# The four z projections of a hybrid block, moved ahead of v heads 1 to 4

## Chip, cores and metric

One Trainium2 chip, one of its cores. The metric is the device time of one execution of the kernel in microseconds (us); smaller is better. The program works on fp32 data with five engines: TensorE (PE, matrix multiplies), VectorE (DVE), ScalarE (ACT), GpSimd (POOL) and SyncE (SP), whose queue issues most of the DMAs.

## The reference, cut to what matters

One layer of a backbone block over 256 latent tokens with a prefix of 256 context tokens, width 1024. A combined projection of the normalised input gives q, k, v, z, a Fourier part f and two sets of gates. A gated delta rule runs over chunks of 64 tokens in both directions, first over the context and then, from the state reached there, over the latent tokens. z only gates the result of that scan, after its norm. A top-4-of-32 mixture of experts ends the block.

```python
q, k, v, a_raw, beta = gdn_inputs(p_ctx, conv_w[l], None)
o_ctx, s_f, s_b = gdn_bidir(q, k, v, a_raw, beta, a_log[l], dt_bias[l], zero, zero)
p = u @ w_in[l]
q, k, v, a_raw, beta = gdn_inputs(p, conv_w[l], rows)
o, _, _ = gdn_bidir(q, k, v, a_raw, beta, a_log[l], dt_bias[l], s_f, s_b)

def merge_branches(p, o, gdn_norm_g, w_fourier_out, w_gdn_out, w_merge_out):
    z = p[..., Z_OFF:F_OFF].astype(jnp.float32).reshape(B, L, NV_HEADS, DV)
    yb = o * lax.rsqrt(jnp.mean(o * o, axis=-1, keepdims=True) + EPS) * gdn_norm_g * jax.nn.silu(z)
    yb = yb.reshape(B, L, V_DIM) @ w_gdn_out
    ya = fourier_mix(p[..., F_OFF:GA_OFF]) @ w_fourier_out
    return (ga * ya + gb * yb) @ w_merge_out
```

## The kernel before

Each fp32 product is made of three TensorE passes over a high and a low part (`mm3`, and the projections, lines 164 to 166). `wsplit` (lines 150 to 158) brings a weight tile in by DMA (`raw`), ScalarE casts its high part (`hi`, line 156) and GpSimd, in most places, subtracts the low part (`lo`, line 157). Each of the three has a ring of three buffers.

The attention part runs in stages. After the k heads comes a loop over eight v heads (`for h in range(8)`): 48 matmuls of 128x256 into one of two `ps_pj` buffers, ten VectorE steps of the short convolution that read this buffer (`conv`, line 394, "taps" from here on), SiLU on ScalarE, four transposes on TensorE (line 572) and a copy. A `ps_pj` buffer is free again when its ten taps are done. Beside it, in program order behind it, VectorE does a triangular solve: 31 steps of a product (line 657) and a subtraction (line 660), then 32x32 transposes (lines 675 and 677). On TensorE the inverse is then put together from small products (lines 691 and 699, twice each, with VectorE's line 702 behind each pair). The first matmul of the state scan (line 748) needs the first half of that.

The scan has two passes (`s` = 0 context, 1 latent) of four chunks and two halves each, 16 half steps, each a chain of TensorE (line 738), VectorE (741), TensorE (748), VectorE (751), TensorE (761) and VectorE (768). In pass 1 lines 776, 781, 787 and 790 write the output as well.

Independent projections fill the gaps. They are written as generators: `fill_q` (q heads 0 to 3, 24 matmuls and eight taps each, and what follows from q), `fill_zf` and `fill_gates`. The first four steps of `fill_zf` are the z projections, two `wsplit`s and 48 matmuls each into a `ps_pf` buffer, with four SiLU calls into `zg`; at the start of its fifth step GpSimd multiplies `zg` by the norm's weight (line 503, two calls), and then come the f projections and their Fourier steps. Three constants say where the steps stand in program order: `ZV[h]` steps of `fill_zf` ahead of v head h, `NZ` steps behind the solve, and `FS[i]` steps of the chain q, z and f, gates in each of the 16 half steps of the scan; `FS` sums to 28, and what is left then runs behind the scan. Program order is not yet the order on an engine: a scheduler places the instructions of each engine, and the order it wrote is what is shown below.

Behind the scan the output is normed (lines 828 to 846), projected (`w_gdn_out`, eight times), merged and routed; then the experts' weights, 384 loads of 1 MB, stream through SP's queue (line 812).

Of the kernel before, what the change touches and what calls it, by code (L numbers as in the profile page):

```python
# [31 lines left out]
EP = 1  # L32
FP = 1
AG = ((2, 2), (2, 1))
ZV = (0, 0, 1, 0, 0, 0, 0, 0)
NKR = 2
BP = (1, 2)
EN1 = 'GG'
EN2 = 'VV'
NZ = 1  # L40
FS = (1, 1, 1, 1, 1, 1, 2, 3, 1, 3, 3, 3, 3, 2, 0, 2)
KOFF, QOFF, VOFF, BOFF, ZOFF, FOFF, GAOFF, GBOFF = 512, 0, 1024, 2048, 2080, 3104, 3616, 4640

# [54 lines left out]
def hybrid_block(es: ExitStack, tc: tile.TileContext, cst, x, c, ctx, c_ctx, w_mod, b_mod, norm1_g, norm2_g, w_in,  # L98
# [29 lines left out]
    def page(name, dtype=F32, tag="pg"):  # L128
        return pg.tile([128, 2048], dtype, name=name, tag=tag, bufs=NPG if tag == "pg" else 2)
# [21 lines left out]
    def wsplit(src, eng, r=None):  # L151
        k = src.shape[1]
        r = r or raw_tile(src)
        hi = rg.tile([128, 1024], F32R, name="hi", tag="hi", bufs=3)
        lo = rg.tile([128, 1024], F32R, name="lo", tag="lo", bufs=3)
        A.copy(hi, r)  # L156
        eng.tensor_tensor(out=lo, in0=r, in1=hi.bitcast(F32), op=ALU.subtract)  # L157
        return [v.rearrange("p (k n) -> p k n", k=k) for v in (hi, lo)]
# [39 lines left out]
    def wcols(off, n, ks=8, k0=0):  # L198
        return kview(w_in[0])[:, k0:k0 + ks, off:off + n]
# [102 lines left out]
    def take(gen, n=1):  # L302
        for _ in range(n):
            next(gen, 0)
# [233 lines left out]
    def factors():  # L538
        bn, bn2, cf = smt("bn", 2, 4, 8), smt("bn2", 2, 4, 8), smt("cf", 2, 4, 8)
        for d in range(2):  # L540
            V.tensor_tensor(out=bn2[:, d].rearrange("p t (h o) -> p t h o", o=2),
                            in0=beta[:, :, 8 * d:8 * d + 8].rearrange("p t (h o) -> p t h o", o=2), in1=byh(nk2), op=ALU.mult)
        nk = smt("nk", 16)
        G.tensor_tensor(out=nk, in0=ssk, in1=mh, op=ALU.pow)
        for d in range(2):
            V.tensor_tensor(out=bn[:, d].rearrange("p t (h o) -> p t h o", o=2),
                            in0=beta[:, :, 8 * d:8 * d + 8].rearrange("p t (h o) -> p t h o", o=2), in1=byh(nk), op=ALU.mult)
        V.scalar_tensor_tensor(out=cf, in0=bn2, scalar=-1.0, in1=egc, op0=ALU.mult, op1=ALU.mult)


        for q, src in enumerate((bn, cf, erest, egc)):
            dv = mix[:, q].rearrange("p (s n) h -> p s n h", s=2)
            sv = [src[:, d].rearrange("p (s t) h -> p s t h", s=2) for d in range(2)]
            G.tensor_copy(dv[0:64, :, 0:4:2, :], sv[0][0:64])
            G.tensor_copy(dv[64:128, :, 1:4:2, :], sv[0][64:128])
            for t in range(2):
                G.tensor_copy(dv[64:128, :, 2 - 2 * t, :], sv[1][64:128, :, t, :])
                G.tensor_copy(dv[0:64, :, 3 - 2 * t, :], sv[1][0:64, :, t, :])

    for h in range(8):  # L560
        if h == FP:
            factors()
        take(fz, ZV[h])
        w = wsplit(wcols(VOFF + 128 * h, 128), G)
# [96 lines left out]

    take(fz, NZ)
    qz = page("qz")
# [585 lines left out]
```

## Time and profile before

| what | us |
| --- | --- |
| median of 3 runs | 1423.77 (1421.94 to 1427.05) |
| the profiled execution | 1422.27 |
| its span, first to last instruction | 1420.4 |
| TensorE busy in the span | 1298.9 |
| VectorE busy in the span | 507.6 |
| GpSimd busy in the span | 270.5 |

The span is cut into stages by the places of their first and last instructions: the v heads and the solve up to 199.1 us, the exit of the solve up to the first state matmul at 221.6, the scan up to 379.8, the norm and transposes behind it up to 400.8, the merge, and from about 470 the experts. A stage's own rows say which engine ends last in it; shares of the whole span are an average over stages with different limits. The clock of TensorE is given as the share of full speed that was granted.

### The profile page before, as it was taken

How to read it: one execution, taken by the hardware profiler on the slowest of the kernel's cores; microseconds unless marked ns; L12 is line 12 of the kernel's file. 1: busy time of each engine (PE TensorE's matmuls, PEld its weight loads, DVE VectorE, ACT ScalarE, POOL GpSimd, SP SyncE). 2: the span in 40 equal slices, each digit the busy share in tenths (PEclk: the TensorE clock that was granted, in tenths of full speed). 3: DMA queues.
4: the chain of work that ended last, by engine and by line, in shares of the span. 5: the costliest groups of instructions: out<-in, count | busy, mean ns of one | idle time of the engine just before them, and what ended most of it. 6: DMA issues, size and time to landing. Idle time of an engine off the chain costs nothing. (4 is left out here: it accounts for less than half of the span.)

```text
span 1420.4 us, 18877 instructions
## 1 busy us (share of the span) xinstructions
PE 1298.9 (91%) x7761; PEld 656.9 (46%) x7761; DVE 507.6 (36%) x965; ACT 243.4 (17%) x434; POOL 270.5 (19%) x248
## 2 busy tenths in 40 slices
PE   4997859899998999999999999999999999999985
PEld 2667858578888443342333333333333232332321
DVE  3579994645567112252111221121121211112112
ACT  3443243233433100000000000000000000000000
POOL 2335336544322301010010000100000001000000
PEclk9999879999989999999999999999999999999997
DMA  9962132134559999999999999999999999999993
GB/s 319 378 258 79 55 89 77 45 90 113 164 199 359 378 421 422 421 419 422 421 421 420 422 421 421 420 421 422 421 422 420 421 421 422 421 420 421 422 421 161
DMA packets 122327, 471.85 MB, mean 332 GB/s; under 512 B 10438, under 2 KB 63918, under 8 KB 71040
## 3 DMA queue, kind: packets, MB, share of 16 engines
q1 hardware_dynamic: 120576, 468.03, 82.9%
q10 hardware_dynamic: 1376, 2.41, 0.6%
q8 instruction: 62, 1.02, 0.3%
q0 software_dynamic: 288, 0.19, 0.2%
q14 instruction: 25, 0.20, 0.0%
HBM read 469.54 MB, written 1.06 MB: 331 GB/s over the span
## 5 line engine op out<-in xcount | busy, mean ns | idle before, releaser
L1114 PE MATMUL ps_gu<-we,xg 128*64 128x512 f32 x2048 | 471.9, 598 | 2.8 <-DMA we<-in_w_up_dram 2.4
L1114 PEld LDWEIGHTS ps_gu<-we,xg 128*64 128x64 f32 x2048 | 140.8, 136 | 297.5 <-issue 274.0
L1137 PE MATMUL ps_dn<-we,aT 128*64 128x512 f32 x1024 | 239.2, 603 | 2.7 <-SPq L1149 2.0
L1103 POOL CAST rowsel<-pick 128x128 fp32r<-128x128 f32 x32 | 9.7, 304 | 685.3 <-PE ps_gu L1115 685.3
L157 POOL TENSOR_TENSOR lo<-raw,hi 128x1024 fp32r<-128x1024 f32 x44 | 108.0, 2457 | 154.2 <-ACT hi L156 143.1
L1146 DVE TENSOR_TENSOR x_pg<-x_pg,ps_st 128x512 f32<-128x512 f32 x128 | 82.5, 684 | 128.2 <-PE ps_st L1144 128.2
L1137 PEld LDWEIGHTS ps_dn<-we,aT 128*64 128x64 f32 x1024 | 67.5, 137 | 124.7 <-issue 114.3
L1120 ACT ACTIVATE sg<-gt 128x512 f32<-128x512 f32 x32 | 20.1, 629 | 439.5 <-DVE gt L1118 412.1
L1122 DVE TENSOR_SCALAR up<-ps_gu 128x512 f32<-128x512 f32 x32 | 22.1, 691 | 201.0 <-PE ps_gu L1115 193.8
L1140 DVE TENSOR_TENSOR ys<-ps_dn,g2r 128x512 f32<-128x512 f32 x32 | 22.1, 692 | 196.6 <-PE ps_dn L1137 191.0
L1144 PE MATMUL ps_st<-ys,wT 64*128 64x512 f32 x256 | 77.1, 649 | 12.8 <-DVE ys L1140 12.0
L156 ACT CAST hi<-raw 128x1024 fp32r<-128x1024 f32 x64 | 67.0, 1047 | 110.5 <-issue 37.3
L164 PE MATMUL ps_pj<-u,hi 128*128 128x256 f32 x224 | 68.1, 307 | 18.3 <-DVE a L394 18.3
L1129 ACT COPY aT<-ps_tp 128x512 f32<-128x512 f32 x32 | 18.8, 586 | 324.6 <-PE ps_tp L1127 324.6
L1086 PEld LDWEIGHTS ps_tp<-oh,h 128*128 128x128 f32 x512 | 64.2, 200 | 14.1 <-issue 13.3
L394 DVE SCALAR_TENSOR_TENSOR a<-ps_pj,cvw,a 128x189 f32<-128x189 f32 (+3 forms) x152 | 63.7, 431 | 17.9 <-ACT a L391 16.1
L1086 PE MATMUL ps_tp<-oh,h 128*128 128x128 f32 x512 | 68.5, 289 | 1.1 <-DVE oh L1073 1.1
L1118 DVE TENSOR_SCALAR gt<-ps_gu 128x512 f32<-128x512 f32 x32 | 22.2, 692 | 128.5 <-issue 95.5
L165 PE MATMUL ps_pj<-u,hi 128*128 128x256 f32 x224 | 67.8, 303 | 0.0
L166 PE MATMUL ps_pj<-u,lo 128*128 128x256 f32 x224 | 66.4, 297 | 0.0
L1124 POOL TENSOR_TENSOR up<-up,sg 128x512 f32<-128x512 f32 x32 | 40.4, 1262 | 98.1 <-DVE up L1123 98.1
L164 PEld LDWEIGHTS ps_pj<-u,hi 128*128 128x128 f32 x224 | 45.2, 203 | 27.5 <-issue 25.5
(348 smaller groups left out, 1634.1 us busy)
## 6 DMA issues: line engine op xcount, KB each, us to landing
we<-in_w_gate_dram SPq DMA_DIRECT2D x128, 1024.0 KB, 19.8
we<-in_w_up_dram SPq DMA_DIRECT2D x128, 1024.0 KB, 19.8
we<-in_w_down_dram SPq DMA_DIRECT2D x128, 1024.0 KB, 19.8
raw<-in_w_in_dram SPq DMA_DIRECT2D x44, 512.0 KB, 4.0
wmb<-in_w_mod_dram SPq DMA_DIRECT2D x16, 1024.0 KB, 12.2
wm<-in_w_mod_dram SPq DMA_DIRECT2D x16, 512.0 KB, 7.4
raw<-in_w_gdn_out_dram SPq DMA_DIRECT2D x8, 512.0 KB, 4.0
raw<-in_w_merge_out_dram SPq DMA_DIRECT2D x8, 512.0 KB, 4.2
```

The costliest lines, as they stand in the source:

```text
L156: A.copy(hi, r)
L157: eng.tensor_tensor(out=lo, in0=r, in1=hi.bitcast(F32), op=ALU.subtract)
L164: mm(out_, sh_, mh_, start=start and i == 0, stop=False)
L165: mm(out_, sh_, ml_, start=False, stop=False)
L166: mm(out_, sl_, mh_, start=False, stop=stop and i == n - 1)
L394: V.scalar_tensor_tensor(out=ov, in0=iv, scalar=wap, in1=ov, op0=ALU.mult, op1=ALU.add)
L1086: mm(p[:, kl * n:(kl + 1) * n], h2[:, t, rows2(k)], oh[:, n * t:n * t + n], start=(t == 0), stop=(t == 1))
L1114: mm(p[64 * g:64 * g + 64, :], xg[:, k, :], w[:, 512 * g:512 * g + 512], start=(k == 0), stop=False)
L1124: G.tensor_tensor(out=up, in0=up, in1=sg, op=ALU.mult)
L1137: mm(p[64 * g:64 * g + 64, :], aT[:, f % 4, 64 * (f // 4):64 * (f // 4) + 64], w[:, 512 * g:512 * g + 512], start=(f == 0), stop=(f == 7))
L1144: mm(p, wT[64 * g:64 * g + 64, t * 128:(t + 1) * 128], ys[64 * g:64 * g + 64, :], start=True, stop=True)
L1146: V.tensor_tensor(out=x_pg[:, t, gsl], in0=x_pg[:, t, gsl], in1=p, op=ALU.add)
```

## The change

The change is in two constants:

```diff
-ZV = (0, 0, 1, 0, 0, 0, 0, 0)
+ZV = (0, 1, 1, 1, 1, 0, 0, 0)
-NZ = 1
+NZ = 0
```

In program order z steps 0 to 3 now stand ahead of v heads 1, 2, 3 and 4. Before, step 0 stood ahead of v head 2, step 1 behind the solve, and steps 2 and 3 in the scan's chain. The chain is two steps shorter, so with the same `FS` the later steps come two steps earlier in the scan, and four instead of six are left behind it. The operations and their number stay the same.

On GpSimd, in the stage of the v heads, the difference reads as follows (`lo` is the low part of a weight tile, `zg` line 503, `bv` line 728 of the scan):

```order
 L557 COPY mix<-bn 64x2x8
 L558 COPY mix<-bn 64x2x8
+L157 TENSOR_TENSOR lo<-raw,hi 128x1024 x8
+L503 TENSOR_TENSOR zg<-zg,gng_b 128x1024 x2
+L157 TENSOR_TENSOR lo<-raw,hi 128x1024 x2
+L728 TENSOR_TENSOR bv<-vtokc,mix 64x512 x2
 L157 TENSOR_TENSOR lo<-raw,hi 128x1024 x4
-L728 TENSOR_TENSOR bv<-vtokc,mix 64x512 x2
-L157 TENSOR_TENSOR lo<-raw,hi 128x1024 x7
-L728 TENSOR_TENSOR bv<-vtokc,mix 64x512 x2
-L157 TENSOR_TENSOR lo<-raw,hi 128x1024 x2
```

Ten low parts, those of z1 to z3 among them, and the two multiplications of `zg` now stand ahead of the first `bv`, where four low parts stood.

At the end of the solve VectorE and TensorE change as follows. On VectorE, before (the `a` tiles are the convolutions: `a_2100` of q head 0, `a_2164` of q head 1; `ps_pj_` names the buffer that a tap reads):

```order
L394 SCALAR_TENSOR_TENSOR a_2100<-ps_pj_2075,cvw_126,a_2100 128x4x63
L660 TENSOR_TENSOR tt_456<-tt_456,prod_1629 128x2x31
L394 SCALAR_TENSOR_TENSOR a_2100<-ps_pj_2075,cvw_126,a_2100 128x4x63
L675 STREAM_TRANSPOSE xt_1628<-tt_456 128x32x32 x2
L677 STREAM_TRANSPOSE xc_1627<-tt_456 128x32x32 x2
L394 SCALAR_TENSOR_TENSOR a_2100<-ps_pj_2075,cvw_126,a_2100 128x3x63
L394 SCALAR_TENSOR_TENSOR a_2164<-ps_pj_2139,cvw_126,a_2164 128x3x63
...
L702 SCALAR_TENSOR_TENSOR ub0_1764<-ps_sc_1844,cs1_75,ub0_1764 128x16x32 x2
```

And now (`a_1725` is v head 6, `a_1801` v head 7, `a_2230` q head 0, `a_2294` q head 1):

```order
L394 SCALAR_TENSOR_TENSOR a_1725<-ps_pj_1675,cvw_126,a_1725 128x4x63
L660 TENSOR_TENSOR tt_456<-tt_456,prod_1824 128x2x31
L394 SCALAR_TENSOR_TENSOR a_1725<-ps_pj_1675,cvw_126,a_1725 128x4x63
L675 STREAM_TRANSPOSE xt_1823<-tt_456 128x32x32 x2
L677 STREAM_TRANSPOSE xc_1822<-tt_456 128x32x32 x2
L394 SCALAR_TENSOR_TENSOR a_1725<-ps_pj_1675,cvw_126,a_1725 128x3x63
L394 SCALAR_TENSOR_TENSOR a_1801<-ps_pj_1751,cvw_126,a_1801 128x255
...
L394 SCALAR_TENSOR_TENSOR a_2230<-ps_pj_2205,cvw_126,a_2230 128x3x63
...
L394 SCALAR_TENSOR_TENSOR a_2294<-ps_pj_2269,cvw_126,a_2294 128x192
L702 SCALAR_TENSOR_TENSOR ub0_1894<-ps_sc_1974,cs1_75,ub0_1894 128x16x32 x2
```

Seventeen taps (three of v head 6, all ten of v head 7 and four of q head 0) have moved from ahead of the transposes to behind them, and between the transposes and the first line 702 there stand 23 taps instead of 11.

On TensorE in the same place, before (one row for each block of projection matmuls; `ps_pf_2518` is z2, `ps_pj_2220` and `ps_pj_2300` are q heads 2 and 3):

```order
L572 MATMUL ps_sc_1619<-cs_74,b_1605 128x128 x4
L691 MATMUL ps_sc_1778<-xt_1628,ah0_449 32x32 x2
...
L164 MATMUL ps_pf_2518<-hi_2521,u10_156 128x256
...
L164 MATMUL ps_pj_2220<-u10_156,hi_2216 128x256
L699 MATMUL ps_sc_1844<-prod_1629,xc_1627 32x32 x64
L691 MATMUL ps_sc_1911<-xt_1628,ah0_449 32x32 x2
...
L164 MATMUL ps_pj_2300<-u10_156,hi_2296 128x256
L699 MATMUL ps_sc_1977<-prod_1629,xc_1627 32x32 x64
L748 MATMUL ps_sc_2050<-bv_2047,ub0_1764 64x128 x8
```

And now (`ps_pj_2205` is q head 0, `ps_pj_2269` q head 1, `ps_pj_2350` q head 2; the last line 572 ahead of line 691 is that of v head 7):

```order
L164 MATMUL ps_pj_2205<-u10_156,hi_2201 128x256
...
L164 MATMUL ps_pj_2269<-u10_156,hi_2265 128x256
L572 MATMUL ps_sc_1814<-cs_74,b_1800 128x128 x4
L691 MATMUL ps_sc_1908<-xt_1823,ah0_449 32x32 x2
...
L699 MATMUL ps_sc_1974<-prod_1824,xc_1822 32x32 x64
L691 MATMUL ps_sc_2041<-xt_1823,ah0_449 32x32 x2
...
L164 MATMUL ps_pj_2350<-u10_156,hi_2346 128x256
L699 MATMUL ps_sc_2107<-prod_1824,xc_1822 32x32 x64
L748 MATMUL ps_sc_2180<-bv_2177,ub0_1894 64x128 x8
```

The 24 matmuls of q head 0 and 9 of q head 1 now stand between the last v projection and line 691; z2 and z3 are gone from the exit and the scan.

Behind the last state matmul of the scan (line 787) TensorE has, before (a row for each gate's block in `ps_pf`):

```order
L787 MATMUL ps_sc_3682<-S_3322,qz_1761 64x256 x4
L164 MATMUL ps_pf_3825<-u10_156,hi_3821 128x256
...
L164 MATMUL ps_pf_3857<-u10_156,hi_3853 128x256
...
L164 MATMUL ps_pf_3889<-u10_156,hi_3885 128x256
...
L840 MATMUL ps_sc_3976<-cs_74,o_2771 128x128 x4
L840 MATMUL ps_sc_3985<-cs_74,o_2771 128x128
L164 MATMUL ps_pf_3921<-u10_156,hi_3917 128x256
```

And now:

```order
L787 MATMUL ps_sc_3746<-S_3386,qz_1891 64x256 x4
L164 MATMUL ps_pf_3889<-u10_156,hi_3885 128x256
...
L164 MATMUL ps_pf_3921<-u10_156,hi_3917 128x256
L840 MATMUL ps_sc_3976<-cs_74,o_2844 128x128 x4
L840 MATMUL ps_sc_3985<-cs_74,o_2844 128x128 x4
```

Two gates (`ps_pf_3825` and `ps_pf_3857`) have moved into the scan: 36 gate matmuls stand behind it instead of 84.

## Rows read from the trace of the kernel before

**Rows 1.** The page: the span, and DMA's busy tenths in 40 equal slices.

```profile
span 1420.4 us, 18877 instructions
...
DMA  9962132134559999999999999999999999999993
```

**Rows 2.** Windows by stage: length, busy time of each engine (instructions), granted clock, DMA share, GB/s.

```profile
133.00:199.10 66.10, 47.87 (x341) 46.51 (x339) 64.65 (x127) 21.18 (x38) 23.34 (x12) 0.85 0.27 73
199.10:221.60 22.50, 15.78 (x571) 14.84 (x570) 15.27 (x24) 10.01 (x18) 8.98 (x5) 0.77 0.25 71
...
297.00:379.80 82.80, 82.80 (x765) 69.58 (x763) 41.33 (x112) 30.63 (x63) 34.53 (x20) 1.00 0.45 122
379.80:400.80 21.00, 18.07 (x125) 16.48 (x123) 15.44 (x33) 9.07 (x25) 9.88 (x5) 0.86 0.63 202
```

**Rows 3.** Windows: the start of the experts' stream and the experts.

```profile
440.00:450.00 10.00, 10.00 (x87) 10.00 (x87) 5.66 (x5) 3.09 (x10) 1.81 (x1) 1.00 1.02 418
...
600.00:1411.00 811.00, 763.67 (x3524) 276.30 (x3519) 168.16 (x263) 55.48 (x95) 57.50 (x78) 1.00 0.99 413
```

**Rows 4.** VectorE's taps in 132 to 199.2, by line: count, busy us, mean ns.

```profile
L394 DVE SCALAR_TENSOR_TENSOR a<-ps_pj,cvw,a 128x189 f32<-128x189 f32 (+3 forms) x65 | 27.1, 430 | 1.1 <-ACT a L391 1.1
```

**Rows 5.** Timeline in the solve (start, duration, engine): VectorE, and GpSimd's two instructions beside them.

```profile
173.29 0.66 DVE L657 TENSOR_TENSOR prod<-tt,xt 128x480 f32<-128x480 f32 x1
173.98 2.74 DVE L660 TENSOR_TENSOR tt<-tt,prod 128x480 f32<-128x480 f32 x1
...
182.47 0.47 DVE L394 SCALAR_TENSOR_TENSOR a<-ps_pj,cvw,a 128x252 f32<-128x252 f32 x1
...
173.71 2.50 POOL L157 TENSOR_TENSOR lo<-raw,hi 128x1024 fp32r<-128x1024 f32 x1 [5.44 <-ACT hi L156]
...
182.58 2.34 POOL L157 TENSOR_TENSOR lo<-raw,hi 128x1024 fp32r<-128x1024 f32 x1 [0.51 <-ACT hi L156]
```

**Rows 6.** Timeline: GpSimd's two multiplications of `zg`, in the scan.

```profile
240.10 4.72 POOL L503 TENSOR_TENSOR zg<-zg,gng_b 128x1024 f32<-128x1024 f32 x2 [0.90 <-ACT zg L500]
```

**Rows 7.** Timeline of VectorE behind the transposes.

```profile
206.83 4.32 DVE L394 SCALAR_TENSOR_TENSOR a<-ps_pj,cvw,a 128x189 f32<-128x189 f32 x11
```

**Rows 8.** Timeline of TensorE: projections behind idle time, the exit, and at full clock.

```profile
188.70 0.55 PE L164 MATMUL ps_pj<-u,hi 128*128 128x256 f32 x1 [9.05 <-DVE a L394]
189.05 0.41 PE L165 MATMUL ps_pj<-u,hi 128*128 128x256 f32 x1
...
191.19 0.41 PE L166 MATMUL ps_pj<-u,lo 128*128 128x256 f32 x1
...
213.68 1.51 PE L691 MATMUL ps_sc<-xt,ah 32*32 32x32 f32 x109 [2.10 <-issue]
215.12 0.58 PE L165 MATMUL ps_pj<-u,hi 128*128 128x256 f32 x1
...
219.20 1.24 PE L699 MATMUL ps_sc<-prod,xc 32*32 32x32 f32 x123
...
221.60 1.09 PE L748 MATMUL ps_sc<-bv,ub 64*64 64x128 f32 x16
...
222.84 0.28 PE L166 MATMUL ps_pj<-u,lo 128*128 128x256 f32 x1
...
224.03 0.28 PE L164 MATMUL ps_pj<-u,hi 128*128 128x256 f32 x1
```

**Rows 9.** Timeline of TensorE in a half step of the scan without fill.

```profile
272.05 1.12 PE L748 MATMUL ps_sc<-rr,ub 64*64 64x128 f32 x16 [0.75 <-DVE rr L741]
274.05 1.14 PE L761 MATMUL ps_sc<-ye,ktok 64*128 64x256 f32 x8 [0.89 <-DVE ye L751]
```

**Rows 10.** Timeline behind the scan: VectorE, GpSimd, TensorE.

```profile
385.84 2.37 DVE L830 SCALAR_TENSOR_TENSOR ms<-ms,epsn 128x8 f32<-128x8 f32 x1
...
385.35 2.84 POOL L157 TENSOR_TENSOR lo<-raw,hi 128x1024 fp32r<-128x1024 f32 x1 [3.35 <-ACT hi L156]
...
394.16 1.52 PE L840 MATMUL ps_sc<-cs,o 128*128 128x128 f32 x5 [2.02 <-DVE o L834]
```

## The prediction, as it was put on record

> **What bounds the kernel now.** I read the experts first. From about 440 us the DMA engines are busy all the time, 0.99 to 1.02 of their share at 413 to 418 GB/s, up to the end [rows 1, 3]. That stream begins when the part ahead of it hands over its buffers, and no operation in it is touched, so I take a microsecond gained or lost ahead of 440 as one gained or lost at the end. Then I read the front by stages, each for the engine that has no idle time left [rows 2]:
>
> - 133 to 199 us, v heads and solve: VectorE is busy 64.65 of 66.10 us, TensorE only 47.87. The solve on VectorE sets the end, and TensorE has 18 us of holes.
> - 199 to 221.6, the exit: no engine is full. It is a chain of transposes, small products and whatever is queued between them, with the clock at 0.77.
> - 297 to 380, the latent scan: TensorE is busy 82.80 of 82.80 us at full clock. There every matmul counts.
> - 380 to 401, norm and transposes: a chain again, with gates as cover.
>
> So z is moved from places where TensorE is short (the scan) to one where it has holes, but where VectorE is full.
>
> **Unit prices.** Projections at full clock start every 0.119 us (224.03 - 222.84, ten apart), behind idle time every 0.214 us (191.19 - 189.05, ten apart); those are the two levels of the clock, 2.4 and 1.2 GHz [rows 8]. A tap costs 4.32/11 = 0.39 us back to back [rows 7]; the 65 in the solve took 27.1 us, 0.42 each [rows 4].
>
> **A, the v heads, solve and exit.** By the order on TensorE 59 more projection matmuls stand ahead of the first state matmul (z3's 48 and 24 of z2, less 13 of q heads that now come later): 59 x 0.119 = 7.0 us. They have cover, the 18 us of holes; without it they would cost those 7.0 us. The weight loads ride in a DMA share of 0.27 [rows 2]; SP's queue has the same loads in another order, and I count nothing for it.
>
> The solve itself: seventeen taps leave VectorE's queue ahead of the transposes, 17 x 0.39 = -6.7 us. Against it stands GpSimd. While a low-part subtraction ran there from 173.71 to 176.21, VectorE's line 660, which takes 0.66 us alone for that size (its sister line 657 at 173.29), took 2.74 us and ended with it; a tap at 182.47, beside another such subtraction, took its usual 0.47 [rows 5]. So a GpSimd instruction beside a product or subtraction of the solve costs VectorE up to 2.08 us. The Trainium skill, page "SBUF — State Buffer", section "Who interferes with whom", states it as a rule: a VectorE instruction with two SBUF inputs contends with a GpSimd instruction that reads SBUF, and whoever issues second waits for the whole of the other; these rows agree, 2.74 us against 0.66.
>
> How many more of these does the solve get? Its first product stands at v head 2's taps in both kernels, and three weight tiles are split ahead. Before, GpSimd then had eight low parts and two `bv` left up to the transposes. Now VectorE is at v head 6 when it transposes, so GpSimd has z3 (two), v4 to v7, q0 and q1, again eight, the two `bv`, and new the two `zg` multiplications, which before stood in the scan and took 4.72 us together [rows 6]. Two more calls cost between 0, both beside taps, and 4.2 us; I take 3, nearer to the full block, since the solve's own operations are most of VectorE's work. The solve ends at -6.7 + 3 = -3.7 us.
>
> The exit gets longer, since the seventeen taps and the q heads now stand in it. From the end of the second transposes to the first state matmul it took 221.60 - 206.83 = 14.8 us [rows 7, 8]. Now, in order: six taps until v head 6's buffer is free for q head 0, 2.4; its 24 matmuls behind idle TensorE, 24 x 0.214 = 5.1; nine of q head 1, 1.1, and four transposes, 0.6 (an estimate, five of those matmuls); line 691, 1.51 x 128/109 = 1.8; fifteen of q head 1, 1.8; line 699, 1.24; idle time and the second line 691 as before, 2.10 + 1.51; 21 of q head 2 at the pace of the block at 215.12 to 219.20, 21 x 0.17 = 3.6; the last line 699 to the state matmul as before, 2.4. Sum 23.6 us, 8.8 more. If the clock is at its upper level by then and the idle time goes, it is 24 x 0.119 = 2.9, 2.5 for the 21, and no 2.10: 18.2, 3.4 more. I take the middle, 20.9, **+6.1**: half of the block behind the idle time before was slow too. A = -3.7 + 6.1 = **+2.4**, between -6.7 + 3.4 = -3.3 and 0 + 8.8, which with more blocks could be higher still (rival 2).
>
> **B, the context scan.** From the first state matmul to the place where the q products begin, TensorE had 86 projection matmuls queued, now 27: 59 x 0.119 = -7.0 us. But two half steps lose their cover altogether, and a bare one waits 0.75 us for VectorE's line 741 and 0.89 us for line 751 [rows 9]: 2 x 1.64 = +3.3. The two `zg` calls leave GpSimd here; nobody waited for them that I find. B = **-3.7**, between -7.0 and -2 (a third bare half step).
>
> **C, the latent scan.** `FS` is unchanged and the chain two steps shorter, so two gates move in from behind the scan: 48 matmuls more between its first and last line 787. TensorE has no hole there [rows 2]: 48 x 0.119 = **+5.7**.
>
> **D, behind the scan.** The same 48 matmuls leave: at most -5.7. But the stage is not bound by them alone: TensorE waited 2.02 us for line 834 at 394.16, whose chain (lines 828, 830, 832, 834) runs through VectorE and GpSimd; line 830 took 2.37 us beside a low-part subtraction [rows 10]. With the gates earlier this subtraction comes ahead of the chain, and that block of about 2.2 us goes; what is late next is the chain itself. D = **-2.2**, between -5.7 and +2.4, one low part of 2.4 us ahead of the second line 832.
>
> **Sum.** 2.4 - 3.7 + 5.7 - 2.2 = +2.2 us on the profiled run's 1422.27, its span of 1420.4 and 1.9 around it: 1424.5. That run is 1.5 us below the median of 1423.77, so as a median I expect **1426.0 us**, 0.15% more. What a measurement of this kernel can tell from no change is about 0.3%, 4.3 us.
>
> **Rivals.**
>
> 1. Faster: the z matmuls are free and the exit is no longer than before. q head 0 would have to run under the transposes, as q heads did before. Then A = -3.7 and D = -5.7, the tail giving back all that the scan takes: -3.7 - 3.7 + 5.7 - 5.7 = -7.4, **1416.4 us**. For it: 18 us of holes, and a tail with its clock at 0.86 [rows 2]. Against it: three of v head 6's taps stand behind the transposes on VectorE, and q head 0 needs their buffer.
>
> 2. Slower: GpSimd holds VectorE in the solve more often than I count. If the solve starts while z1 and z2 are still being split, four more low parts fall into it beside the two `zg`, six in all at 2.08 = 12.5 instead of 3 us: 2.2 + 9.5 = +11.7, **1435.5 us**. It decides from the third full block on: 3 x 2.08 = 6.2, which makes the sum +5.4. For it: the row at 173.98 and a solve that is dense once the taps are gone [rows 5]; against it: the ring of three buffers lets GpSimd run only so far ahead. The rule cited above is this rival's: by it, every such call that meets a product of the solve holds it up.
>
> That the change doesn't do what it says is excluded by the order on the engines; what is open is only the time.
>
> **How the numbers follow.** My forecast, that A's gain is eaten by its exit and C's loss mostly met by B and D, gets 0.55, with its own range 1420 to 1433 from the bounds of the exit (-2.7, +2.7), of the tail (-3.5, +4.6) and of the two calls (-3, +1.2), which don't all fall on one side. Rival 1 gets 0.15, rival 2 0.27, the rest (another clock in the exit, a fetch of the experts that starts otherwise) 0.03. Of the forecast's 0.55 I put 0.39 within 0.3%, 0.12 slower, 0.04 faster; of rival 1 0.12 faster and 0.03 within; of rival 2 0.26 slower and 0.01 within; the rest one part each. That is faster 0.17, same 0.44, slower 0.39. The range reaches from between rival 1 and the forecast's lower end to rival 2: 1415 to 1437.
>
> **What would show it.** Right: the transposes (line 675) start some 4 us earlier; the first state matmul comes 2 to 3 us later, with q head 0's block right behind the transposes at about 0.2 us a matmul; the sixth line 738 is within 2 us of before; the last line 787 is 4 to 6 us later, TensorE full between; the first projection of `w_gdn_out` 1 to 4 us later. Wrong: more than four of lines 657 and 660 beyond before's number above 2 us (rival 2); a first state matmul earlier than before (rival 1); a latent scan as long as before would fell C, and a stream of the experts that doesn't shift with the front would fell the base of the sum.

## The result and the profile after

The changed kernel takes **1433.38 us** (median of 8 runs, 1430.08 to 1436.46), the kernel before on the same chip 1422.86 us (1419.23 to 1427.05). The ratio is 1.0073, with an interval of 1.0059 to 1.0087: slower by 10.5 us. Two of the seven runs of experiment 2 below were in a slow state, at a lower clock (2184 and 4645 us), and are left out of its figures; all other runs were fast. The forecast was 1426.0 with a range of 1415 to 1437, so the time lies in the range, on the side of rival 2's 1435.5.

The profiled execution took 1435.58 us, 2.2 above its median; that of before is 0.6 below the 1422.86. The stages below therefore add up to a little more than the medians do. The page of after:

```profile
span 1433.8 us, 18866 instructions
...
DMA  9963322123648999999999999999999999999994
```

The experts' stream is as dense as in [rows 1] and starts later. The windows of after by the same stages as in [rows 2] (length, busy time of PE, PEld, DVE, ACT, POOL with instructions, granted clock, DMA share, GB/s):

```profile
133.00:204.30 71.30, 47.31 (x351) 46.34 (x349) 70.55 (x116) 21.15 (x39) 31.59 (x13) 0.86 0.27 78
204.30:235.10 30.80, 18.55 (x589) 17.73 (x589) 20.43 (x36) 12.89 (x24) 9.13 (x5) 0.72 0.22 60
304.00:396.20 92.20, 92.20 (x840) 77.34 (x836) 45.11 (x124) 34.35 (x69) 36.05 (x21) 1.00 0.45 122
```

VectorE is still full in this stage (70.55 of 71.30 us), which grew by five microseconds instead of shrinking; GpSimd's part went from 23.34 to 31.59. The stage of the exit grew from 22.5 to 30.8. The latent scan is full as before, and longer.

Two lines mark the scan's end and the start of the routing: 787, the last state matmul, and 885, the first of the router's transposes. Their summaries give count, shortest, median and longest in ns, and the first and the last start; of before, then of after:

```profile
L787 PE MATMUL ps_sc<-S,qz x64: 379/379/431, 293.7 to 379.4; 128*64 128x256 f32 x64
L885 PE MATMUL ps_sc<-cs,h x16: 271/272/328, 438.0 to 454.9; 128*128 128x128 f32 x16
```

```profile
L787 PE MATMUL ps_sc<-S,qz x64: 379/379/430, 304.3 to 395.9; 128*64 128x256 f32 x64
L885 PE MATMUL ps_sc<-cs,h x16: 271/272/328, 450.9 to 467.9; 128*128 128x128 f32 x16
```

With the first state matmul at 221.60 [rows 8] and at 235.20 (below), the terms of the sum measure as follows (all between starts):

| term | stage | before | after | measured | forecast |
| --- | --- | --- | --- | --- | --- |
| A | up to the first state matmul | 221.6 | 235.2 | +13.6 | +2.4 |
| B | from there to the first line 787 | 72.1 | 69.1 | -3.0 | -3.7 |
| C | first to last line 787 | 85.7 | 91.6 | +5.9 | +5.7 |
| D | from there to the first line 885 | 58.6 | 55.0 | -3.6 | -2.2 |
| | front, sum | 438.0 | 450.9 | +12.9 | +2.2 |
| | from line 885 to the end of the span | 982.4 | 982.9 | +0.5 | 0 |

B, C and D add up to -0.7 (forecast -0.2). The whole miss is A, and it has two halves.

**The solve.** The transposes (line 675) start at 204.29 instead of 199.45: +4.8, where -3.7 was forecast. VectorE's lines from 104 us to there, before (count, busy us, mean ns; idle time before):

```profile
L394 DVE SCALAR_TENSOR_TENSOR a<-ps_pj,cvw,a 128x189 f32<-128x189 f32 (+3 forms) x83 | 34.6, 430 | 1.3 <-ACT a L391 1.1
L657 DVE TENSOR_TENSOR prod<-tt,xt 128x62 f32<-128x62 f32 (+15 forms) x31 | 24.9, 803 | 0.1
L660 DVE TENSOR_TENSOR tt<-tt,prod 128x62 f32<-128x62 f32 (+15 forms) x31 | 21.5, 692 | 0.2
...
L650 DVE SCALAR_TENSOR_TENSOR xc<-ah,cs 128x1024 f32<-128x1024 f32 x2 | 2.6, 1276 | 0.0
```

and after:

```profile
L657 DVE TENSOR_TENSOR prod<-tt,xt 128x62 f32<-128x62 f32 (+15 forms) x31 | 29.8, 960 | 0.4
L394 DVE SCALAR_TENSOR_TENSOR a<-ps_pj,cvw,a 128x189 f32<-128x189 f32 (+3 forms) x66 | 27.5, 430 | 0.2
L660 DVE TENSOR_TENSOR tt<-tt,prod 128x62 f32<-128x62 f32 (+15 forms) x31 | 21.9, 708 | 0.3
...
L650 DVE SCALAR_TENSOR_TENSOR xc<-ah,cs 128x1024 f32<-128x1024 f32 x2 | 8.1, 4080 | 0.0
```

The seventeen taps did leave (83 to 66, -7.1 us of listed time; by the trace eighteen left, five of q head 0 and not four: 125 taps start ahead of the transposes before, 107 after). But lines 657 and 660 together take 51.7 us instead of 46.4, +5.3, and the two lines 650, which bring the system into place ahead of the solve, 8.1 instead of 2.6, +5.5. So the solve itself, from the first line 657 to the transposes, is as long as before (66.3 us against 66.4): what the missing taps gave it, the longer steps took, and it starts 5.0 us later. VectorE and GpSimd at that place in after (between them the summary of line 650, in ns):

```profile
125.44 8.08 DVE L650 SCALAR_TENSOR_TENSOR xc<-ah,cs 128x1024 f32<-128x1024 f32 x2
```

```profile
L650 DVE SCALAR_TENSOR_TENSOR xc<-ah,cs x2: 1275/4080/6885, 125.4 to 132.3; 128x1024 f32<-128x1024 f32 x2
```

```profile
124.17 7.07 POOL L157 TENSOR_TENSOR lo<-raw,hi 128x1024 fp32r<-128x1024 f32 x3
...
160.17 5.50 POOL L503 TENSOR_TENSOR zg<-zg,gng_b 128x1024 f32<-128x1024 f32 x2
```

Three low parts run back to back (one of v, two of z). The first line 650 stands beside all three, 6.89 us, and ends 1.1 us behind the third; the second then takes its usual 1.28. The mean of 4.08 hides that. The second GpSimd row is the `zg` pair. Before, one low part had just ended, at 125.76, when the first line 650 began:

```profile
123.39 2.37 POOL L157 TENSOR_TENSOR lo<-raw,hi 128x1024 fp32r<-128x1024 f32 x1
```

```profile
125.83 1.28 DVE L650 SCALAR_TENSOR_TENSOR xc<-ah,cs 128x1024 f32<-128x1024 f32 x1
```

Beside the `zg` pair of after stand two operations of the solve, at a full block each:

```profile
160.90 2.53 DVE L660 TENSOR_TENSOR tt<-tt,prod 128x480 f32<-128x480 f32 x1
...
163.68 2.51 DVE L657 TENSOR_TENSOR prod<-tt,xt 128x494 f32<-128x494 f32 x1
```

**The exit.** From the end of the second transposes to the first state matmul it takes 235.20 - 211.71 = 23.5 us instead of 221.60 - 206.96 = 14.6. TensorE of after (a busy time, then the idle time before it and what ended it):

```profile
213.80 0.55 PE L164 MATMUL ps_pj<-u,hi 128*128 128x256 f32 x1 [10.42 <-DVE a L394]
...
220.18 1.29 PE L691 MATMUL ps_sc<-xt,ah 32*32 32x32 f32 x128
...
223.36 1.53 PE L699 MATMUL ps_sc<-prod,xc 32*32 32x32 f32 x126
...
228.36 0.85 PE L691 MATMUL ps_sc<-xt,ah 32*32 32x32 f32 x42 [2.69 <-issue]
...
233.91 1.35 PE L699 MATMUL ps_sc<-prod,xc 32*32 32x32 f32 x128
235.20 1.09 PE L748 MATMUL ps_sc<-bv,ub 64*64 64x128 f32 x16
```

and the same engine before, where line 691 came:

```profile
201.42 0.32 PE L691 MATMUL ps_sc<-xt,ah 32*32 32x32 f32 x4 [2.13 <-DVE xt L675]
203.25 1.92 PE L691 MATMUL ps_sc<-xt,ah 32*32 32x32 f32 x124 [1.51 <-DVE xt L675]
```

Before, line 691 ran while VectorE was still transposing for line 699: it starts 2.0 us behind the start of line 675. After, it starts 15.9 us behind, because q head 0's matmuls stand ahead of it, and these wait 10.42 us for a buffer whose last taps stand behind the transposes. VectorE of after in that stretch:

```profile
204.29 3.77 DVE L675 STREAM_TRANSPOSE xt<-tt 128x1024 f32<-128x1024 f32 x2
207.94 3.77 DVE L677 STREAM_TRANSPOSE xc<-tt 128x1024 f32<-128x1024 f32 x2
211.58 5.23 DVE L394 SCALAR_TENSOR_TENSOR a<-ps_pj,cvw,a 128x189 f32<-128x189 f32 x13
220.56 3.70 DVE L394 SCALAR_TENSOR_TENSOR a<-ps_pj,cvw,a 128x189 f32<-128x189 f32 x8 [3.74 <-ACT a L391]
...
225.63 1.40 DVE L702 SCALAR_TENSOR_TENSOR ub<-ps_sc,cs,ub 128x512 f32<-128x512 f32 x2
```

### The profile page after: what moved, and what is told of

The parts are those of the page before. It is cut to its first block, busy times and chain, and to the rows that moved or that the text cites. A ratio compares the mean times of both kernels' runs of the same rounds, so it can differ in the third digit from the quotient of the medians.

```text
span 1433.8 us, 18866 instructions
## 1 busy us (share of the span) xinstructions
PE 1298.4 (91%) x7761; PEld 656.5 (46%) x7761; DVE 517.7 (36%) x965; ACT 244.0 (17%) x434; POOL 272.4 (19%) x248
## 5 line engine op out<-in xcount | busy, mean ns | idle before, releaser
L1144 PE MATMUL ps_st<-ys,wT 64*128 64x512 f32 x256 | 77.0, 645 | 12.8 <-DVE ys L1140 12.0
```

The costliest lines, as they stand in the source:

```text
L1144: mm(p, wT[64 * g:64 * g + 64, t * 128:(t + 1) * 128], ys[64 * g:64 * g + 64, :], start=True, stop=True)
```

## The experiments

The theory: (1) GpSimd's instructions hold VectorE in lines 650, 657 and 660; (2) line 691 queues behind a q head that waits for taps; (3) C and D are as forecast. The rivals: the z matmuls themselves, or the `zg` pair alone, make the loss; a bare scan makes it; or the buffers of `ps_pj` do. Twelve kernels, all timed against the kernel before on the same chip.

**1. The gates back behind the scan** (after, one constant; the sixteen entries sum to 26):

```diff
-FS = (1, 1, 1, 1, 1, 1, 2, 3, 1, 3, 3, 3, 3, 2, 0, 2)
+FS = (1, 1, 1, 1, 1, 1, 0, 3, 1, 3, 3, 3, 3, 2, 0, 2)
```

> The changed kernel with FS[6] = 0 instead of 2, so that the Fourier and gate steps stand in the same half steps of the scan as in the kernel before, and six steps are left behind the scan. If the longer latent scan is the 48 gate matmuls that came in from behind it, the stretch from the fifth line 738 to the last line 787 falls from 114.4 us back to 108.5, and the stretch from there to the first line 885 grows again by about 3.5: 2.4 us less in all, about 1431.0. If the latent scan is longer for another reason (buffers, the state's updates), nothing changes: 1433.4.

Measured 1435.55 us, 1.0086 (1.0066 to 1.0105). In its own stage it does as expected: line 787 runs for 85.7 us again (91.6 in after), and from its last start to the first line 885 it is 58.8 us instead of 55.0. That confirms C. The 2.1 us that this gives do not show in the total: in the profiled run the solve started 1.5 us later, the exit took 23.9 us, and the context scan up to the q products 42.3 instead of 39.5, at a granted clock of 0.92 instead of 1.00. The edit does not touch the context scan, and experiment 2, whose context scan is that of after too, has the same 42.3 us at 0.92. So the 39.5 of after's one profile is not what this order always takes.

**2. Without the `zg` pair** (after, line 503 left out):

```diff
-        for t in range(2):
-            G.tensor_tensor(out=zg[:, t, :].rearrange("p (h n) -> p h n", h=8), in0=zg[:, t, :].rearrange("p (h n) -> p h n", h=8),
-                            in1=bc3(gng_b, 8, 128), op=ALU.mult)
```

> The changed kernel without GpSimd's two multiplications of zg by the norm's weight (line 503; the output lacks that weight). Theory that GpSimd holds VectorE in the solve: the two solve operations that ended with them, 2.53 and 2.51 us, go back to some 0.65, the transposes (line 675) come 3.7 us earlier and the time is about 1429.7. Theory that only the queue behind the transposes counts: 1433.4, the transposes where they were.

Measured 1430.40 us (median of five), 1.005 (1.0032 to 1.0068). The transposes start at 200.56 instead of 204.29, -3.7, and lines 657 and 660 fall from 51.7 to 47.6: two calls, two full blocks of 2.05 each. Of the 3.7 us, 0.9 stand ahead of the solve, which starts that much earlier in this run; the solve itself is 2.8 us shorter. Line 650 stays at 8.1 and the exit at 24.5. Each against the kernel before on its own chip, 0.50% are left of 0.73%: the pair is about a third of the loss, as far as intervals that overlap can tell.

**3. z without its low parts** (after; the high part stands in, so eight GpSimd calls go and the matmuls stay):

```diff
-    w = wsplit(wcols(ZOFF + 256 * g, 256, 4, 4 * kq), G)
+    w = wsplit(wcols(ZOFF + 256 * g, 256, 4, 4 * kq), G, low=False)
```

> The changed kernel without GpSimd's eight low parts of the z weights: the high part stands in for the low part, so all matmuls are there and z is less exact. Theory that GpSimd holds VectorE: line 650, 8.1 us for two in the changed kernel, goes back to about 2.6, and the two products of the solve at 2.5 and 2.3 us that stood beside z3's low parts go to 0.4; the transposes come some 9 us earlier, the time is about 1424.5. Theory that the taps and q projections in the exit are the whole loss: 1433.4.

Line 650 is back at 2.5 us, the transposes start at 195.55, -8.7, with all 192 matmuls of z in place. So the matmuls are covered and GpSimd is what holds VectorE. Not all of the 8.7 us is the change's own: line 474, ahead of line 650, takes 5.8 us here and 9.7 in before and after alike, so it was held in both. The exit stays long, 23.1. The whole time, 1465.83 us, can't be compared: other values of z route other tokens, and the kernel has 7905 matmuls instead of 7761 and takes 1021.0 us from line 885 to the end instead of 982.9. The expected total missed that; ahead of the routing, line 885 comes 6.1 us earlier than in after.

**4. GpSimd's cost by itself** (before, with four unused multiplications of the size of a low part, one behind each of v heads 2 to 5; nobody reads their output):

```diff
+        if 1 < h < 6: G.tensor_tensor(out=dmy.rearrange("p (h n) -> p h n", h=8), in0=bc3(vtok[0][:, 0, h * 128:(h + 1) * 128], 8, 128), in1=bc3(gng_b, 8, 128), op=ALU.mult)
```

> The kernel before with four more GpSimd multiplications of 128x1024 elements that nobody uses, one behind each of v heads 2 to 5 (each about 2.4 us, the size of a low part). Theory that GpSimd holds VectorE in the solve: up to 2.1 us for each, the stretch from the first line 657 to the transposes grows from 66.4 us by 4 to 8, and the time is 1427 to 1431. If GpSimd's instructions cost VectorE nothing, the time is that of before, 1422.9.

Measured 1430.04 us, 1.0045 (1.0032 to 1.0058), as the theory said. Lines 657 and 660 in this kernel:

```profile
L657 DVE TENSOR_TENSOR prod<-tt,xt 128x62 f32<-128x62 f32 (+15 forms) x31 | 27.0, 872 | 0.2
L660 DVE TENSOR_TENSOR tt<-tt,prod 128x62 f32<-128x62 f32 (+15 forms) x31 | 26.9, 868 | 0.3
```

53.9 us instead of 46.4, and ten of them above 2 us instead of six: 1.9 us for each block more, nearly the 2.08 of the prediction. The stretch from the first line 657 to the transposes grows from 66.4 to 71.8 us, within what was expected. It is not quite four calls and nothing else: by the trace the solve has two low parts and five taps fewer than before, and of the 7.2 us of the total some is in the exit (15.3 us) and the context scan (44.2).

**5. Half the change: z0 and z1 only** (after):

```diff
-ZV = (0, 1, 1, 1, 1, 0, 0, 0)
+ZV = (0, 1, 1, 0, 0, 0, 0, 0)
```

> A part of the change alone: z0 and z1 ahead of v heads 1 and 2, z2 and z3 in the scan as before, none behind the solve; the scan's chain is that of the kernel before. By the order, 16 taps stand between the transposes and line 702 (11 before, 23 in the changed kernel) and only q head 1's last matmuls ahead of line 691. Theory that the exit's queue costs: exit of 15 to 17 us instead of 23.4. Theory that GpSimd holds VectorE: line 650 is blocked if three low parts run back to back there as in the changed kernel, +5.5, and no zg in the solve. Both: 1424 to 1429; a time of 1433 would fell both.

Measured 1423.06 us, 0.9998 (0.9984 to 1.0011). Line 650 is as slow as in after (7.9) and the solve starts as late (137.90), but only five low parts are left in it, lines 657 and 660 fall to 41.8 and the transposes start at 199.96. The exit is 14.6. The time is 1 us below what was expected; both statements on the stages held in the main (line 650 is blocked, the exit is not longer).

**6. The other half: z1, z2, z3 behind the solve** (before):

```diff
-NZ = 1
+NZ = 3
```

> The other part of the change alone: the kernel before with NZ = 3, so that z2 and z3 stand behind the solve with z1 instead of in the scan; z0 stays ahead of v head 2. By the order 120 taps stand ahead of the transposes (125 before, 108 in the changed kernel). The latent scan gains 48 gate matmuls as in the changed kernel: +5.5 us there, -3.3 behind it, -3 in the context scan, whichever theory holds. Theory of the exit's queue: exit 18 to 20 us, +4. Theory of GpSimd: solve longer by up to 4 us if z2's low parts fall into it. Together 1424 to 1430; were it 1433 the v heads' part of the change would cost nothing.

Measured 1423.28 us, 0.9986 (0.9963 to 1.001). This has B, C and D in it (line 787 runs for 92.4 us), and a solve as late as that of after (transposes at 203.82 against 204.29; lines 657 and 660 at 50.7). The exit was expected at 18 to 20 us. But its line 691 starts 4.3 us behind line 675, its exit is 13.4 us, shorter than before, and line 885 comes at 440.2 instead of 450.9. Of these 10.8 us the exit is 10.1. (The profiled execution was the longest of its ten, by the time behind line 885, which is not used here.)

**7. The low parts of half the change on VectorE** (z0 and z1 only, as in 5, and):

```diff
-    w = wsplit(wcols(ZOFF + 256 * g, 256, 4, 4 * kq), G)
+    w = wsplit(wcols(ZOFF + 256 * g, 256, 4, 4 * kq), V if g < 2 else G)
```

> z0 and z1 ahead of v heads 1 and 2 as in p1_z01, with their four low parts made by VectorE (1.2 us each) instead of GpSimd. Theory that GpSimd holds VectorE: line 650 goes back from 8.1 us for two to 2.6 or 4.5, the four low parts cost VectorE 4.9, of which two lie ahead of the solve's path; the time is 1420 to 1424. Rival, that the blocks are cheaper than the work: 1426.

Measured 1423.04 us, 0.9997 (0.9983 to 1.001): no gain. Line 650 falls only to 6.6, since its first instruction still stands beside three low parts of GpSimd back to back (122.30 to 129.39), and the low parts of z0 and z1 now cost VectorE their own time.

**8. Three buffers for `ps_pj`** (after; `ps_sc` gives one up):

```diff
-    _nb = {"pj": 2, "pf": 2, "sc": 4}
+    _nb = {"pj": 3, "pf": 2, "sc": 3}
```

> The changed kernel with three ps_pj buffers instead of two, and three ps_sc instead of four. By the order all four q projections then stand ahead of line 691, and a q head needs no buffer that the taps behind the transposes still read. Theory that the exit is long because q head 0 waits for v head 6's last taps and runs behind idle TensorE: the exit falls from 23.5 us to 15 or 17, the time to about 1426. If only the clock makes the exit long, it stays above 20, and the time about 1433; a ps_sc buffer less can cost the scan something in both.

The exit falls to 13.5 us, less than in before. The time does not: 1444.34 us, 1.0136 (1.0109 to 1.0162). The order moved the q heads up into the solve: 133 taps start ahead of the transposes (107 in after), 12 low parts in the solve (8), and the transposes start at 227.75. Moved, not removed; the expected time missed that. VectorE is already 4.7 us later at line 464, ahead of all this; whether the missing `ps_sc` buffer does that is not shown.

**9. The exit of after with the solve of before** (after, z0 and z1 ahead of v heads 2 and 3):

```diff
-ZV = (0, 1, 1, 1, 1, 0, 0, 0)
+ZV = (0, 0, 1, 1, 0, 0, 0, 0)
```

> z0 and z1 ahead of v heads 2 and 3, z2 and z3 in the scan as before, none behind the solve. By the order this kernel has the changed kernel's queue at the exit (24 matmuls of q head 0 and 21 of q head 1 ahead of line 691, 111 taps ahead of the transposes, 23 between them and line 702), but the kernel before's GpSimd order ahead of line 650, no zg in the solve and the kernel before's scan. Theory of the exit's queue: line 650 at 2.6 us, the transposes 4 to 6 us earlier than before (14 taps fewer), the exit 23 us instead of 14.6, the scan as before: 1425 to 1427. If the exit of the changed kernel was long only because the solve ended late, the exit here stays at 15 us and the time falls to 1418.

This has as many z projections in the scan as before, line 650 at 2.6, no `zg` in the solve, and transposes at 196.28, 3.2 earlier than before. Still it takes 1431.68 us, 1.0053 (1.004 to 1.0067). Its order has 45 matmuls of q heads 0 and 1 ahead of line 691, and the last 21 of them wait for a tap behind the transposes:

```profile
209.18 0.55 PE L164 MATMUL ps_pj<-u,hi 128*128 128x256 f32 x1 [14.31 <-DVE a L394]
...
214.51 1.29 PE L691 MATMUL ps_sc<-xt,ah 32*32 32x32 f32 x128
```

The exit is 23.9 us, 9.3 longer than before, behind a solve that ends earlier than before. The total came out above what I expected because the context scan is 5.8 longer too, up to the q products (line 606): 148 projection matmuls stand in it instead of 134 (14 x 0.119 = 1.7), TensorE waits once for 2.1 us ahead of a line 748, and the clock is at 0.96; the last two I did not expect.

**10. z0 and z1 ahead of v heads 2 and 4** (after):

```diff
-ZV = (0, 1, 1, 1, 1, 0, 0, 0)
+ZV = (0, 0, 1, 0, 1, 0, 0, 0)
```

> z0 ahead of v head 2 as before, z1 ahead of v head 4, z2 and z3 in the scan as before. By the order 120 taps ahead of the transposes, 16 between them and line 702, and 24 of q head 1's matmuls ahead of line 691: an exit like that of p1_z01, 14.65 us. Theory that GpSimd holds VectorE: without three low parts back to back at line 650 this kernel saves the 5.5 us that p1_z01 lost there: 1417 to 1421, a version faster than both. Rival, that p1_z01's line 650 delayed nothing in the end: 1423.

Measured 1422.64 us, 0.9999 (0.9988 to 1.001): the same as before, not the gain I hoped for. Its line 691 starts 2.1 us behind line 675 and its exit is 12.2 us, 2.4 shorter; the context scan, with 147 matmuls, gives 3.7 back.

**11. The four z a head later** (after):

```diff
-ZV = (0, 1, 1, 1, 1, 0, 0, 0)
+ZV = (0, 0, 1, 1, 1, 1, 0, 0)
```

> The changed kernel with its four z projections one v head later, ahead of heads 2 to 5. Exit queue (24 and 21 matmuls, 110 taps ahead of the transposes, 24 behind), zg in the solve, scan and tail as in the changed kernel; ahead of line 650 GpSimd's order is that of before. Theory that GpSimd holds VectorE at line 650: 8.1 us for two go back to 2.6, the time is about 1428. Rival, that the low parts only move into the solve and block as much there: 1433.

Measured 1434.77 us, 1.0065 (1.0041 to 1.0088). Line 650 is free of GpSimd again:

```profile
L660 DVE TENSOR_TENSOR tt<-tt,prod 128x62 f32<-128x62 f32 (+15 forms) x31 | 29.1, 940 | 0.4
L657 DVE TENSOR_TENSOR prod<-tt,xt 128x62 f32<-128x62 f32 (+15 forms) x31 | 26.9, 869 | 0.3
L650 DVE SCALAR_TENSOR_TENSOR xc<-ah,cs 128x1024 f32<-128x1024 f32 x2 | 2.5, 1274 | 0.0
```

and the solve starts at 133.38. But what line 650 gave back lines 657 and 660 took (56.0 us), and the transposes start at 204.16, within 0.2 us of after. The low parts cost the same in either place. (Of its four runs one took 1426.86 us, the others 1433.85 to 1436.11.) The exit is 25.9.

**12. q heads 0 and 1 in the buffers of `ps_pf`** (after):

```diff
-            p = P("pj")
+            p = P("pf" if h < 2 else "pj")
```

> The changed kernel with q heads 0 and 1 projected into the two ps_pf buffers instead of ps_pj, so that q head 0's 24 matmuls no longer wait for the taps of v head 6 that stand behind the transposes. By the order the solve keeps its GpSimd work and has about as many taps ahead of the transposes; ahead of line 691 stand 25 other projection matmuls with nothing to wait for, and 39 taps stand between the transposes and the first line 702 (23 in the changed kernel). My theory (the exit is long because q head 0 waits 10.4 us for that buffer): the transposes stay at 203 to 206 us, no idle time of TensorE on line 394 is left in the exit, and it falls from 23.5 to 14 to 18 us; the whole time falls to 1424 to 1428. Rival (the exit is long because of the number of matmuls and taps that stand in it, whatever they wait for, and the low clock): the exit stays at 21 us or more and the time at 1431 to 1436.

Neither statement held: 1440.11 us, 1.0117 (1.0099 to 1.0135), transposes at 207.17, an exit of 30.5. The wait for taps was not removed; it doubled:

```profile
214.94 0.55 PE L164 MATMUL ps_pj<-u,hi 128*128 128x256 f32 x1 [10.90 <-DVE a L394]
...
223.61 0.58 PE L164 MATMUL ps_pf<-hi,u 128*128 128x256 f32 x1 [3.06 <-DVE a L394]
...
229.99 1.29 PE L691 MATMUL ps_sc<-xt,ah 32*32 32x32 f32 x128
```

With 39 taps between the transposes and line 702, q head 2 waits for v head 6's buffer, and the next step of the z and f chain for that of a q head; both stand ahead of line 691. That is the same mechanism one step further, though the run was not the removal that I meant it to be, and so does not tell the wait from the matmuls behind it.

**All kernels together.** For the exit one number divides the runs: how long behind the start of line 675 line 691 starts. In before and in experiments 4 to 8 and 10 no projection ahead of line 691 starts later than the transposes on a wait for a tap; line 691 starts 2.0 to 4.3 us behind line 675, and the exits are 12.2 to 15.3 us. In after and in experiments 1 to 3, 9, 11 and 12 one or two do; line 691 starts 15.9 to 22.8 us behind, and the exits are 23.1 to 30.5 us. There is nothing between. The number of matmuls does not divide them: by the traces 24 to 27 projection matmuls start between the transposes and line 691 in experiments 4, 5 and 8, with nothing to wait for, and 21 in experiment 9, behind a wait of 14.31 us. Nor does a wait by itself: in experiment 10 a `ps_pj` block waits 7.39 us for a tap too, but starts 6.7 us ahead of the transposes, and the exit is the shortest of all. So it is a wait that ends behind the transposes. What the wait costs by itself and what the lower clock behind it adds, no run separates.

## Why the prediction was right, and where it was wrong

The time fell in the range and the chance for slower was 0.39, but the likeliest case, within 0.3%, did not come; the sum was 10.7 us short of the profile, and all of that lies in A. The upper end of the range came from rival 2, not from the forecast, whose own range ended at 1433; that the time lies in it is in part luck.

- **The solve, -3.7 forecast, +4.8 measured. This is the step that failed.** It had three faults. First, I counted GpSimd's blocks only in lines 657 and 660 and never asked what else VectorE does with two inputs in SBUF. Line 650 does, and it stands ahead of the solve on the path: +5.5 us with no term in the sum. Second, "two calls more, 3 us" took low parts and the `zg` pair as if their number alone mattered; lines 657 and 660 grew by 5.3. Experiment 2 puts 4.1 of that on the pair, two full blocks; I had put 3, between none and both. Third, the taps were worth less: where one stands between other operations, its listed 0.40 us overlaps the next instruction, which starts 0.33 us later, as in after at 202.92 and 203.25. By the starts in the trace the taps that left gave 6.4 us (eighteen at 0.36; the sum had seventeen at 0.39, 6.7). From the first line 464 to the transposes, each instruction counted up to the next one's start, it adds up: VectorE 0.4 us later at line 464, lines 650 +5.6, lines 657 and 660 +6.2 (more than their listed +5.3, since fewer taps overlap them), taps -6.4, idle time -0.7, the rest -0.3, together +4.8 as measured. The prediction's reading of the block itself was right but for a detail: line 660 at 173.98 ended 0.5 us behind the low part, not with it.

```profile
202.92 0.40 DVE L394 SCALAR_TENSOR_TENSOR a<-ps_pj,cvw,a 128x189 f32<-128x189 f32 x1
203.25 0.20 DVE L657 TENSOR_TENSOR prod<-tt,xt 128x62 f32<-128x62 f32 x1
```

- **The exit, +6.1 forecast, +8.9 measured.** The mechanism was right, and so was the chain: I worked out 23.6 us for it at the lower clock, and it took 23.5. q head 0 starts 2.1 us behind the transposes (forecast 2.4), line 691 at 8.5 (9.2), line 699 at 11.6 (12.8), the gap ahead of the second line 691 is 2.69 (2.10). What was mis-sized is the choice of half of the way to full clock, though the row it was modelled on [rows 8, at 188.70] showed a block behind 9 us of idle time at 0.214 a matmul, and here there were 10.42 us. The granted clock of the stage is 0.72, below the 0.77 of [rows 2]. That the slow sum meets the time so closely is partly luck: of q head 0's matmuls only the first fifteen start 0.21 us apart and the others 0.12, and four transposes (line 572) more stand among them than the sum has; all 21 of q head 2 run at 0.21, where 0.17 was put; and from the last line 699 to the state matmul it is 1.3 us instead of 2.4. Experiment 9 shows the exit's cost without the rest, 6 its absence with the rest.
- **A as a whole.** My range for it went from -3.3 to 8.8, and it measured 13.6. It held rival 2's mechanism, GpSimd in the solve, and the slow exit as if only one of them could come; both came. Lines 657 and 660 stand above 2 us ten times instead of six, four more, just short of the sign I named for rival 2; its cost came all the same, half of it in line 650. Rival 2's 1435.5 is near the measured time, but it has 9.5 us more than the forecast in the solve and nothing more in the exit, where the runs show 8.5 and 2.8; and its reason, four more low parts in the solve, did not come: eight start there, against nine before (the prediction counts eight in both).
- **B, -3.7 forecast, -3.0 measured.** Right in this profile: 75 instead of 134 projections up to the q products, 59 fewer as the prediction says (it counts 27 and 86), and 2.8 us more of bare waits on lines 741 and 751, for which I had put 3.3. In the profiles of experiments 1 and 2, with the clock at 0.92 instead of 1.00 in the context scan, B is 71.3 us, only 0.8 less than before.
- **C, +5.7 forecast, +5.9 measured.** Right, and experiment 1 takes it back to 85.7 us by one constant.
- **D, -2.2 forecast, -3.6 measured.** Right in sign and nearly in size, but not by the row I named. The second line 830 is still held by a low part:

```profile
402.34 2.31 DVE L830 SCALAR_TENSOR_TENSOR ms<-ms,epsn 128x8 f32<-128x8 f32 x1
...
406.39 2.19 DVE L834 SCALAR_TENSOR_TENSOR o<-o,ms,zg 128x128 f32<-128x128 f32 x8 [0.22 <-POOL ms L832]
```

What went is the block on the second line 834, 2.19 us here; before it took 4.28, beside the next low part, which no longer stands there. The block at 385.84 [rows 10] stays, at 2.31. VectorE and GpSimd of before:

```profile
390.88 4.28 DVE L834 SCALAR_TENSOR_TENSOR o<-o,ms,zg 128x128 f32<-128x128 f32 x8 [1.20 <-POOL ms L832]
```

```profile
391.56 2.39 POOL L157 TENSOR_TENSOR lo<-raw,hi 128x1024 fp32r<-128x1024 f32 x1 [0.72 <-DVE o L834]
```

- **The base of the sum** held: the stream of the experts shifted by the 12.9 us of the front, and no more than 0.5 was added behind. (Over the other profiles that stretch varies by some microseconds, 978.9 to 988.9 us without experiment 3, so a single profile does not give the total to better than that.)

The signs named in the prediction read: transposes 4.8 us later (4 earlier was the sign for right), the first state matmul 13.6 later (2 to 3), q head 0 behind the transposes at about 0.2 us a matmul (as named, for its first fifteen), the sixth line 738 10.6 later (within 2), the last line 787 16.5 later (4 to 6), the first projection of `w_gdn_out` 11.7 later (1 to 4), the latent scan 5.9 longer (as named). Every sign that counts from the start of the span says that A was wrong; those of single stages came.

What stays open: why the granted clock in the context scan is 1.00 in after's profile and 0.92 in those of experiments 1 and 2; what holds one line 748 of experiments 9 and 10 for 2.1 and 1.9 us; and why the first line 650 of after gets no turn between the three low parts, while in experiment 12 the two lines 650, beside two low parts, take 2.18 and 3.42 us.

## What to carry to other kernels

When work is moved to a stage that one engine fills, go through that engine's whole list there and ask of every operation what the moved work's helpers do to it, not only of the one whose slow copy the trace happens to show; the cost then does not go away by moving the helpers inside the stage. When a chain has to pass through an in-order queue, look for what stands ahead of its first link and what that waits for: here independent matmuls made the exit nine microseconds longer, not by their number but because their buffer was freed behind the chain's own step. And where two rivals rest on different mechanisms, their sum belongs in the range.

## What the runs showed of the hardware

A GpSimd subtraction or multiplication of 128x1024 beside a VectorE operation with both inputs in SBUF costs VectorE 1.9 to 2.1 us (experiments 2 and 4). Three of them back to back held one line 650 for 6.89 us instead of 1.28, and cost GpSimd nothing: they took 7.07 us, 2.36 each, their usual time. In the solve, where VectorE and GpSimd alternate, both lose: the two multiplications of `zg` took 5.50 us instead of the 4.72 of [rows 6]. Taps, which read one of their two inputs from PSUM, keep a mean of 426 to 432 ns in the solve of every kernel, whatever GpSimd does. The Trainium skill, page "SBUF — State Buffer", section "Who interferes with whom", has both as a rule: a VectorE instruction with two SBUF inputs contends with a GpSimd instruction that reads SBUF, and one with at most one SBUF input, outside its 2-port modes, does not. The traces agree, for scalar_tensor_tensor (line 650: 6.89 us against 1.28) as for tensor_tensor (line 657: 2.51 us at 163.68).

What I had not expected is how fully the cost is kept: the low parts and the two multiplications, shared out differently over lines 650, 657 and 660 in after and in experiment 11, gave transposes at 204.29 and 204.16 us.
